# Sums of squares of the RMS norms: two float32r matmuls of a split operand in the place of one float32 matmul

## The chip, the cores and the metric

The kernel runs on one core of one Trainium2 chip. The core has a matrix engine (TensorE, shown as PE for its matmuls and PEld for the weight loads that go with them), a vector engine (VectorE, DVE), a scalar engine (ScalarE, ACT), GpSimd (POOL) and a queue engine (SyncE, SP) that issues most transfers. Matmuls write to PSUM, which has eight banks of 512 float32 columns; the rest works in SBUF, whose tiles have 128 partitions.

The metric is the device time of one execution in microseconds (us), as a median over runs. Before the change it is 1512.06 us (three runs, 1512.05 to 1512.68).

## The reference, cut to what matters

A two-layer transformer-like trunk on one sequence of 512 tokens with 1024 features. Each layer is a mixer, a cross-attention over a memory of 256 tokens, and a gated feed-forward block. What the change touches is the RMS norm that stands before each of these, over the memory, inside the mixers' heads, and at the end:

```python
def rms_norm(x, gain):
    x32 = x.astype(jnp.float32)
    y = x32 * lax.rsqrt(jnp.mean(x32 * x32, axis=-1, keepdims=True) + RMS_EPS)
    return (y * gain.astype(jnp.float32)).astype(x.dtype)
...
for layer in range(DEPTH):
    xn = rms_norm(x, mix_norm[layer])
    mixed = ...                              # layer 0: forgetting + differential attention; layer 1: mLSTM
    x = x + mixed
    x = x + memory_cross_attention(rms_norm(x, xattn_norm[layer]), rms_norm(mem, mem_norm[layer]), ...)
    x = x + conv_ffn(rms_norm(x, ffn_norm[layer]), ...)
return rms_norm(x, final_norm)
```

In layer 0 each of the four differential heads is normed over its 128 values, in layer 1 each of the four mLSTM heads over its 256 values.

## The kernel before, in words

**Layout.** The activations are held with features on partitions and tokens along the free dimension: `x` is eight tiles of 128 features by 512 tokens. So a norm is a sum over partitions and over the eight tiles. The tiles' squares are made on ScalarE and added up on VectorE into one tile `sq` (128x512; `squares`, L461 to L470). The sum over its partitions is a matmul. In `rsqrt_cols` (L390 to L396) each block of 128 tokens of `sq` is loaded as the weights, and a 128x2 tile of ones, `ones2`, is the moving operand; two equal columns of sums of 128 tokens come out in a PSUM bank. `rsqrt` (L398 to L411) makes the inverse root with some twelve VectorE instructions on 128x4 numbers: scale and epsilon (`z`, L404), a first guess from the bits, and three Newton steps (L408 to L410). `bcast_cols` (L413 to L435) spreads the result over all partitions: it splits it into two parts (L419 and `sub`, L259), builds two 128x512 diagonal tiles `sqt` on VectorE (L424), and multiplies them with ones on TensorE (L430), after which ScalarE copies the bank to `rb` (L434), where the caller wants it in SBUF. Projections run on the un-normed tiles meanwhile; `rb` multiplies their outputs when they leave PSUM.

**Precision.** Projections are exact to near float32 by splitting: `split` (L261) copies a value to float32r on ScalarE (the high part, L262), and VectorE subtracts it from the value (the low part, L259, also float32r). A product is then three float32r matmuls, high by high, high by low and low by high (`mm3`, L268 to L270; L329 to L331 in token-major form). Weights are split in this way as they arrive, 128x1024 at a time. The sums of squares are not split: `sq` and `ones2` are float32, and TensorE gets a float32 matmul. Attention scores times values and the mLSTM products are float32 too.

**Order.** Two planners written in Python decide at build time in which order the work is written down. `Plan` (L60) serves the mixers and the cross-attention: items carry a cost on TensorE, a priority, dependencies, resources (PSUM banks, weight buffers) and a chain of costs on ScalarE ("A") and VectorE ("D"); at each point the first ready item by priority goes next. `p_norm` (L347) adds a norm as two items: `one` (the sums and the inverse root) and `two` (the spread and what follows, `fin`). `x_norm` (L360) is that for `x`, and the memory norm, the four heads of layer 0 and the four of layer 1 call `p_norm` as well. `Sched` (L139) serves the feed-forward block with a queue per engine; its `norm` (L1186) adds `sums` (TensorE), `root` (VectorE) and `spread` (TensorE) with due times. The first norm of all (`first_sums`, L455) and the last (`finish`, L1683, through `rsqrt_cols`) are written out by hand. A scheduling layer below the planners then puts the instructions of each engine in their final order, by priority and by when it takes their operands to be ready, so that single broadcast matmuls (L430) stand inside a run of projection matmuls. Each engine executes its own list in order; semaphores make one engine wait for another.

**Where norms end up.** In layer 0's mixer the heads' results go to the output projection that begins after all heads. In layer 1's mixer the norm of `x` comes first, and a chain of small VectorE and ScalarE steps on 4x512 gate rows follows from `rb` (L552 to L587, with the scans L574 and L1464); TensorE's first use of that chain is a small transpose (L1473, of `cv` made at L1462). The last mLSTM head's norm is followed at once by the output projection, which multiplies by that head's split result (tiles `v`, made at L1619).

Of the kernel before, what the change touches and what calls it, by code (L numbers as in the profile page):

```python
# [10 lines left out]
F32R = mybir.dt.float32r  # L11
# [5 lines left out]
P = 128  # L17
SEQ = 512
# [41 lines left out]
class Plan:  # L60
# [11 lines left out]
    def add(self, fn, dur=0.0, deps=(), prio=None, take=(), free=(), chain=(), pre=(), after=0.0, order=(), load=(), st=None):  # L72
        it = Item(fn, dur, [d for d in deps if d is not None], len(self.items) if prio is None else prio, take, free, chain, pre, after, order, load, st)
        it.n = len(self.items)
        self.items.append(it)
        return it
# [141 lines left out]
class Builder:  # L218
# [128 lines left out]
    def p_norm(self, pl, state, n, done, scale, eps, fin, deps=(), prio=None, after=0.0, fdeps=(), chain=(("A", 0.5),)):  # L347

        st = {}

        def one():
            st["r"] = self.rsqrt_cols(state["sq"], n, scale, eps)

        def two():
            fin(st["r"], self.bcast_cols(st["r"], n, *done))

        a = pl.add(one, 0.4 * n / 512, deps, prio, take=("s",), free=("s",), chain=(("D", 2.3),), after=after)
        return pl.add(two, 0.5 * n / 512, [a, *fdeps], prio, take=("s",), free=("s",), chain=chain)

    def x_norm(self, pl, prio=0, after=0.0, deps=()):  # L360
# [22 lines left out]
    def evac_tok(self, ps, r, hi, lo):  # L383
# [2 lines left out]
        nc.scalar.activation(hi, ps, AF.Identity, scale=r)  # L386
        nc.vector.scalar_tensor_tensor(out=lo, in0=ps, scalar=r, in1=hi.bitcast(F32), op0=ALU.mult, op1=ALU.subtract)


    def rsqrt_cols(self, sq, n, scale, eps):  # L390

        nt = n // P
        ps = self.bank("b")
        for t in range(nt):
            self.nc.tensor.matmul(ps[:, 2 * t : 2 * t + 2], sq[:, t * P : (t + 1) * P], self.ones2[:], start=True, stop=True)  # L395
        return self.rsqrt(ps, nt, scale, eps)  # L396
# [722 lines left out]
    def ffn_steps(self, layer, mp):  # L1119
# [3 lines left out]
        nc, t = self.nc, self.t  # L1123
        sc = Sched(raw=3, h=3, s2=1, s4=1, a22=1, sum=1, hs=2, c=1, dr=2, v=1, u2=1, u3=1, act=10, acc=4, s=2, w=2)
        add = sc.add
# [4 lines left out]
        state = {}  # L1130
# [4 lines left out]
        def pe(dur, fn, deps, take=(), free=()):  # L1135
            clock[0] += dur
            return add("PE", dur, fn, deps, clock[0] - dur, take, free, 0.2)
# [48 lines left out]
        def norm():  # L1186
            prev = self.state
            st = {}
            n = {}

            def sums():
                n["ps"] = self.bank("s")
                for i in range(4):
                    nc.tensor.matmul(n["ps"][:, 2 * i : 2 * i + 2], prev["sq"][:, i * P : (i + 1) * P], self.ones2[:], start=True, stop=True)

            def root():
                self.r = self.rsqrt(n["ps"], 4, 1.0 / DM, EPS)

            def spread():
                self.rb = self.bcast_cols(self.r, SEQ, self.sp, "rb", 1)  # L1200

            a = pe(0.5, sums, (), [("s", st)])
            b = add("DVE", 2.3, root, [a], a.prio, (), [("s", st)])
            s2 = {}
            c = pe(0.5, spread, [b], [("s", s2)], [("s", s2)])
            return add("ACT", 0.7, None, [c], c.prio)
# [75 lines left out]
        def plain(p, fill):  # L1282
            st = {}
            at = clock[0]
            get = rows(st, at + 5.0)
            ready = []
            for j in range(2):
                b, last = block(t["up"][layer, 22 * j + p], KB8, own, clock[0], "acc", (), 2)

                def evac(j=j, b=b):  # L1290
                    nc.vector.tensor_tensor(out=st["hs_"][:, j, 2:514], in0=b["ps"][:], in1=self.rb[:], op=ALU.mult)

                if p == 0 and j == 0:
                    nonlocal normed
                    normed = norm()
                ready.append([add("DVE", 0.69, evac, [last, get, normed], clock[0] + 2.0, (), [("acc", b)])])
                fill()
            tail(p, st, ready, clock[0] + 3.0)
# [136 lines left out]
        if layer == 0:  # L1435
            for m in range(8):
                e = down(4, m, 2)
                a = add("ACT", 1.43, lambda m=m: self.xprep(m, "mix", 1, state), [e], clock[0] + 3.0)
# [368 lines left out]
```

## Time and profile before

| | |
|---|---|
| median of three runs | 1512.06 us (1512.05 to 1512.68) |
| profiled execution | 1512.78 us |
| its span in the trace | 1511.0 us |
| TensorE clock granted | 0.998 of full |
| TensorE busy | 1500.0 us (99%) |
| weight loads busy | 1281.7 us (85%) |
| VectorE busy | 1160.1 us (77%) |
| ScalarE busy | 774.8 us (51%) |
| GpSimd busy | 44.0 us (3%) |
| DMA | 146.52 MB, 97 GB/s in the mean |

The span runs from the first to the last instruction of the trace; the execution's own time is 1.8 us longer. Ends of matmuls are modelled, so that TensorE's 99% says that it hardly ever had nothing under way, not that it ran at its peak: what a matmul costs in a stream is the distance from its start to the start of the next. Matmul and weight load are separate records. A "form" such as `128*128 128x2 f32` is 128 rows by 128 columns of weights and an output of 128x2.

In time, by where the sums of the norms stand on TensorE: layer 0's mixer with its output projection takes the span up to 272 us, its cross-attention up to 420, its feed-forward block up to 774, layer 1's mixer up to 1003, its cross-attention up to 1151, and the rest is its feed-forward block with the final norm.

### The profile page before, as it was taken

What the parts mean: (1) busy time and instruction counts of PE and PEld (TensorE: products, weight loads), DVE (VectorE), ACT (ScalarE), POOL (GpSimd) and SP (SyncE); (2) the same over time, 40 slices, a digit from 0 to 9 for tenths busy, and PEclk for the clock granted to TensorE, in tenths of its full rate; (3) what the DMA queues carried; (4) which work ended last, traced back from release to release, by engine and by line L of the source; (5) the groups of instructions that cost most, each with busy time, mean ns of one, the idle gap of its engine ahead of it and who ended that gap; (6) DMA issues with size and microseconds to landing.
All of it is one profiled execution on the core that took longest, in us unless ns stands there. A gap on an engine that the chain in (4) does not pass through costs nothing.

```text
span 1511.0 us, 21313 instructions
## 1 busy us (share of the span) xinstructions
PE 1500.0 (99%) x8026; PEld 1281.7 (85%) x8026; DVE 1160.1 (77%) x2155; ACT 774.8 (51%) x1282; POOL 44.0 (3%) x118
## 2 busy tenths in 40 slices
PE   9999999999999999999999999999999999999998
PEld 8888888888888888988888778888888888888887
DVE  7889885766699788897678857666557988889864
ACT  6768564444465444454446634444445554444444
POOL 2000120000000000000001100000000000000000
PEclk9999999999999999999999999999999999999999
DMA  5222233323223333232222222332323332333322
GB/s 179 84 71 84 84 103 108 112 96 100 95 101 100 97 108 109 84 112 88 81 90 84 80 89 93 99 101 99 111 84 109 108 94 95 98 103 106 102 60 77
DMA packets 47480, 146.52 MB, mean 97 GB/s; under 512 B 5649, under 2 KB 5649, under 8 KB 47377
## 3 DMA queue, kind: packets, MB, share of 16 engines
q1 hardware_dynamic: 46368, 144.04, 29.4%
q8 instruction: 63, 1.03, 0.3%
q10 hardware_dynamic: 1008, 1.12, 0.2%
q14 instruction: 41, 0.33, 0.1%
HBM read 143.04 MB, written 2.10 MB: 96 GB/s over the span
## 4 chain that ended last, share of the span: by engine, by line
PE 92%; DVE 3%; ACT 2%; issue 1%; DMA 1%; POOL 0%; SPq 0%; DVEq 0%; POOLq 0%; ACTq 0%
PE acc L268 19%; PE acc L269 19%; PE acc L270 19%; PE w L269 5%; PE w L268 5%; PE w L270 5%; PE acc L330 2%; PE acc L331 2%; PE acc L329 2%; PE s L268 2%; PE s L269 2%; PE s L270 2%; PE w L1595 1%; PE w L681 1%; PE s L395 1%
## 5 line engine op out<-in xcount | busy, mean ns | idle before, releaser
L268 PE MATMUL acc<-xh,wh 128*128 128x512 f32 (+1 forms) x944 | 356.9, 378 | 0.0
L270 PE MATMUL acc<-xh,wl 128*128 128x512 f32 (+1 forms) x944 | 352.8, 374 | 0.0
L269 PE MATMUL acc<-xl,wh 128*128 128x512 f32 (+1 forms) x944 | 352.6, 374 | 0.0
L259 DVE TENSOR_TENSOR wl<-raw,wh 128x1024 fp32r<-128x1024 f32 (+2 forms) x215 | 258.0, 1200 | 51.9 <-ACT wh L262 38.1
L262 ACT CAST wh<-raw 128x1024 fp32r<-128x1024 f32 (+2 forms) x137 | 140.9, 1030 | 168.5 <-PE acc L269 99.6
L270 PEld LDWEIGHTS acc<-xh,wl 128*128 128x128 f32 x944 | 177.5, 188 | 31.7
L268 PEld LDWEIGHTS acc<-xh,wh 128*128 128x128 f32 x944 | 177.6, 188 | 30.4
L269 PEld LDWEIGHTS acc<-xl,wh 128*128 128x128 f32 x944 | 177.7, 188 | 30.3
L1254 DVE SCALAR_TENSOR_TENSOR c<-hs,vec,c 128x512 f32<-128x512 f32 x176 | 128.4, 746 | 7.4 <-ACT c L1247 6.8
L269 PE MATMUL w<-al,wh 128*128 128x512 f32 x304 | 118.5, 390 | 0.0
L268 PE MATMUL w<-ah,wh 128*128 128x512 f32 x304 | 118.5, 390 | 0.0
L270 PE MATMUL w<-ah,wl 128*128 128x512 f32 x304 | 118.3, 389 | 0.0
L1159 ACT CAST wh<-raw 128x1024 fp32r<-128x1024 f32 (+1 forms) x60 | 61.3, 1022 | 77.8 <-PE acc L269 49.3
L1247 ACT ACTIVATE c<-hs,vec 128x512 f32<-128x512 f32 x88 | 70.0, 812 | 40.2 <-DVE hs L1393 23.5
L495 DVE TENSOR_TENSOR x<-w,x 128x512 f32<-128x512 f32 x72 | 49.5, 687 | 31.9 <-PE w L270 31.6
L270 PEld LDWEIGHTS w<-ah,wl 128*128 128x128 f32 x304 | 57.1, 188 | 12.0
L268 PEld LDWEIGHTS w<-ah,wh 128*128 128x128 f32 x304 | 57.1, 188 | 10.9
L269 PEld LDWEIGHTS w<-al,wh 128*128 128x128 f32 x304 | 57.1, 188 | 10.7
L1159 ACT CAST wh<-dr 128x512 fp32r<-128x512 f32 x64 | 39.7, 620 | 47.9 <-issue 17.4
L1268 ACT CAST ah<-c 128x512 fp32r<-128x512 f32 x44 | 27.3, 620 | 68.9 <-DVE c L1264 68.9
L330 PE MATMUL acc<-wl,xh 128*128 128x256 f32 (+1 forms) x192 | 61.9, 323 | 0.2 <-DVE wl L259 0.2
L329 PE MATMUL acc<-wh,xh 128*128 128x256 f32 (+1 forms) x192 | 61.7, 326 | 0.0
(373 smaller groups left out, 3323.4 us busy)
## 6 DMA issues: line engine op xcount, KB each, us to landing
raw<-in_up_dram SPq DMA_DIRECT2D x88, 512.0 KB, 3.3
dr<-in_down_dram SPq DMA_DIRECT2D x64, 256.0 KB, 2.6
raw<-in_xk_dram SPq DMA_DIRECT2D x16, 512.0 KB, 3.3
raw<-in_wo_dram SPq DMA_DIRECT2D x16, 512.0 KB, 3.2
raw<-in_xq_dram SPq DMA_DIRECT2D x16, 512.0 KB, 3.3
raw<-in_xv_dram SPq DMA_DIRECT2D x16, 512.0 KB, 3.3
raw<-in_xo_dram SPq DMA_DIRECT2D x16, 512.0 KB, 3.3
raw<-in_down_dram SPq DMA_DIRECT2D x16, 384.0 KB, 3.0
```

Source lines behind the costliest of these rows:

```text
L259: self.nc.vector.tensor_tensor(out=lo, in0=v, in1=hi.bitcast(F32), op=ALU.subtract)
L262: self.nc.scalar.copy(hi, v)
L268: mm(out, wh, xh, start=first, stop=False, skip_group_check=parts)
L269: mm(out, wh, xl, start=False, stop=False, skip_group_check=parts)
L270: mm(out, wl, xh, start=False, stop=last, skip_group_check=parts)
L329: mm(ps, xh[k][:, ts], wh[:, ws], start=(k == 0), stop=False)
L330: mm(ps, xh[k][:, ts], wl[:, ws], start=False, stop=False)
L331: mm(ps, xl[k][:, ts], wh[:, ws], start=False, stop=(k == 7))
L495: self.nc.vector.tensor_tensor(out=self.x[m][:], in0=ps[:], in1=self.x[m][:], op=ALU.add)
L1159: nc.scalar.copy(st["wh"][:, :cols], st[tag][:, :cols])
L1247: nc.scalar.activation(st["c_"][:, j, :], hs()[:, j, 2:514], AF.Identity, scale=self.col("cw", (layer * 3 + 2) * 44 + blk), bias=self.col( ...
L1254: nc.vector.scalar_tensor_tensor(out=c, in0=hs()[:, j, n : n + 512], scalar=w, in1=c, op0=ALU.mult, op1=ALU.add)
```

## The change

The operand `sq` is split as the projections' operands are: `square_parts` makes two new single-buffered 128x512 tiles, `sqh` (ScalarE copy to float32r) and `sql` (VectorE subtraction). `part_sums` then gives for each block of 128 tokens two float32r matmuls into the same two columns, `sqh` and then `sql` as weights, with two columns of the float32r tile of ones `onesr` as the moving operand. In `p_norm` the split is an item `halved` of its own ahead of `one`, with a chain of a ScalarE and a VectorE cost, and `one` costs 0.5 instead of 0.4; in the feed-forward block a ScalarE task, an empty VectorE task and the sums stand in that order. The first norm and the two halves of the last still use float32. Last, `Bacc` is told a scratch size for dynamic DMA of 1024 bytes; without the argument it is 16384 bytes of each SBUF partition.

```diff
         st = {}
 
+        def halved():
+            st["sq"] = self.square_parts(state["sq"], n)
+
         def one():
-            st["r"] = self.rsqrt_cols(state["sq"], n, scale, eps)
+            st["r"] = self.rsqrt(self.part_sums(st["sq"], n, self.bank("b")), n // P, scale, eps)
...
-        a = pl.add(one, 0.4 * n / 512, deps, prio, take=("s",), free=("s",), chain=(("D", 2.3),), after=after)
+        a = pl.add(halved, 0, deps, prio, chain=(("A", 0.1 + 0.47 * n / 512), ("D", 0.14 + 0.54 * n / 512)), after=after)
+        a = pl.add(one, 0.5 * n / 512, [a], prio, take=("s",), free=("s",), chain=(("D", 2.3),), after=after)
         return pl.add(two, 0.5 * n / 512, [a, *fdeps], prio, take=("s",), free=("s",), chain=chain)
...
+    def square_parts(self, sq, n):
+
+        parts = [self.til(self.sp, tag, dtype=F32R, bufs=1) for tag in ("sqh", "sql")]
+        hi, lo = (p[:, :n] for p in parts)
+        self.split(hi, lo, sq[:, :n])
+        return hi, lo
+
+    def part_sums(self, parts, n, ps):
+
+        for t in range(n // P):
+            for i, p in enumerate(parts):
+                self.nc.tensor.matmul(ps[:, 2 * t : 2 * t + 2], p[:, t * P : (t + 1) * P], self.onesr[:, :2], start=i == 0, stop=i == 1)
+        return ps
...
+            def halved():
+                n["sq"] = self.square_parts(prev["sq"], SEQ)
+
             def sums():
-                n["ps"] = self.bank("s")
-                for i in range(4):
-                    nc.tensor.matmul(n["ps"][:, 2 * i : 2 * i + 2], prev["sq"][:, i * P : (i + 1) * P], self.ones2[:], start=True, stop=True)
+                n["ps"] = self.part_sums(n["sq"], SEQ, self.bank("s"))
...
-            a = pe(0.5, sums, (), [("s", st)])
+            a = add("ACT", 0.6, halved, (), 0.0)
+            a = add("DVE", 0.7, None, [a], 0.0)
+            a = pe(0.5, sums, [a], [("s", st)])
...
-    nc = _bacc.Bacc("TRN2", target_bir_lowering=False, num_devices=1)
+    nc = _bacc.Bacc("TRN2", target_bir_lowering=False, num_devices=1, dynamic_dma_scratch_size=1024)
```

## The prediction

> **What bounds the kernel now.** I read the page first, then the stretches, the sums' own lines, the timeline around them and the waits.
>
> ```profile
> span 1511.0 us, 21313 instructions
> ...
> PE 1500.0 (99%) x8026; PEld 1281.7 (85%) x8026; DVE 1160.1 (77%) x2155; ACT 774.8 (51%) x1282; POOL 44.0 (3%) x118
> ...
> PE 92%; DVE 3%; ACT 2%; issue 1%; DMA 1%; POOL 0%; SPq 0%; DVEq 0%; POOLq 0%; ACTq 0%
> ```
>
> TensorE is never long without work and carries 92% of the chain that ended last. So what counts is (a) the distance between matmul starts, where the change alters matmuls, and (b) new waits of TensorE. VectorE and ScalarE have room in the mean; by stretch (PE, PEld, DVE, ACT, POOL busy):
>
> ```profile
> 40.00:230.00 190.00, 189.06 (x1132) 161.04 (x1132) 157.93 (x480) 131.19 (x293) 18.07 (x32) 1.00 0.27 88
> 420.00:775.00 355.00, 355.00 (x1938) 308.58 (x1938) 298.81 (x451) 171.82 (x245) 2.79 (x23) 1.00 0.31 97
> 775.00:840.00 65.00, 64.29 (x278) 50.30 (x278) 50.44 (x89) 40.32 (x62) 6.59 (x12) 1.00 0.26 82
> ```
>
> Outside the start and the end TensorE idles 0.9 us in layer 0's heads and 0.7 us in layer 1's gate chain, and nothing in a feed-forward block. There is little to win from shorter waits, and any real wait put into this stream is lost.
>
> **The change, part by part. 1: the matmuls.** The sums' records:
>
> ```profile
> L395 PEld LDWEIGHTS s<-ones,sq x40: 186/192/192, 164.4 to 1502.7; 128*128 128x128 f32 x40
> L395 PEld LDWEIGHTS s<-ones,tb x32: 188/192/192, 99.7 to 155.1; 128*128 128x128 f32 x32
> L395 PEld LDWEIGHTS s<-ones,hsq x32: 188/192/192, 842.4 to 954.3; 128*128 128x128 f32 x32
> ...
> L1194 PEld LDWEIGHTS s<-ones,sq x16: 186/192/192, 420.0 to 1151.9; 128*128 128x128 f32 x16
> ```
>
> Four mLSTM heads of four token blocks give 16 float32 matmuls in the program and 32 `hsq` records here: one float32 matmul is two loads and two matmuls. The projections' float32r lines have one record for each. So 56 float32 matmuls (13 norms of four blocks, two memory norms of two) are 112 records now, and 112 float32r matmuls will be 112 records. What does one cost?
>
> ```profile
> 115.68 0.19 PEld L330 LDWEIGHTS acc<-wl,xh 128*128 128x128 f32 x1
> 115.80 0.19 PEld L331 LDWEIGHTS acc<-wh,xl 128*128 128x128 f32 x1
> ...
> 115.92 0.98 PEld L395 LDWEIGHTS s<-ones,tb 128*128 128x128 f32 x8
> ...
> 116.83 0.19 PEld L268 LDWEIGHTS acc<-xh,wh 128*128 128x128 f32 x1
> ```
>
> Eight float32 loads take 0.91 us from 115.92 to 116.83, 0.114 each: with two moving columns the load is the cost. Float32r loads just before are 0.12 apart, with 256 moving columns behind each, so a float32r load takes no more than 0.12. From below, the load's length by columns:
>
> ```profile
> L395 PEld LDWEIGHTS s<-ones,sq 128*128 128x128 f32 x40 | 5.2, 191 | 1.1 <-PE s L1657 0.4 <-issue 0.2 <-DVE sq L470 0.2
> ...
> L905 PEld LDWEIGHTS w<-pt,v 128*64 128x64 f32 x64 | 5.0, 136 | 4.8 <-issue 3.5 <-DVE sm L664 0.2
> ...
> L542 PEld LDWEIGHTS w<-xh,wh 128*100 128x100 f32 x8 | 1.3, 164 | 0.5
> ...
> L542 PEld LDWEIGHTS w<-xh,wh 128*40 128x40 f32 x8 | 0.9, 116 | 0.3
> ```
>
> Float32: (191 - 136) / 64 = 0.86 ns a column. Float32r: (164 - 116) / 60 = 0.80. The same rate within the rows' rounding, so 128 columns take between 0.102 and 0.12 us in float32r against 0.110 to 0.114. Over 112 records the difference lies between -1.3 and +1.0 us; I take 0. The matmuls are what the change is about, and they cost the same.
>
> A rule speaks otherwise. The Trainium skill, "FP8 and Floating Point Precision", section "TensorE Precision Notes", says that true float32 makes four passes through the array. By that alone two single passes would halve the sums' array work. The rows differ: with two moving columns the passes vanish beside the load, and the load is paid twice either way.
>
> **2: the split.** One copy on ScalarE and one subtraction on VectorE, as here:
>
> ```profile
> L259 DVE TENSOR_TENSOR al<-c,ah 128x512 fp32r<-128x512 f32 x44 | 30.3, 690 | 14.3 <-ACT ah L1268 13.8
> ...
> L1268 ACT CAST ah<-c 128x512 fp32r<-128x512 f32 x44 | 27.3, 620 | 68.9 <-DVE c L1264 68.9
> ```
>
> Thirteen times 0.62 and 0.69, and half of that twice for the memory: 8.7 us on ScalarE and 9.7 on VectorE, beside TensorE's stream. That costs nothing while the sums are not reached before `sql` is there; without this cover each norm would cost up to 0.62 + 0.69 and two handovers of some 0.07, 1.45 us.
>
> **3: the order.** Both planners know the longer chain and put the sums later. The built orders (no time is in them) show the same matmuls otherwise, moved about in layer 0's mixer from its third head on and in layer 1's mixer; a cross-attention and a feed-forward block differ only at their norm. Where cover is thin:
>
> *Cross-attentions.* 12 matmuls of 512 columns are drawn ahead of the sums. At 0.227 us (below) that is 2.7 us against 1.45: covered, 0. *Feed-forward norms.*
>
> ```profile
> 419.25 0.69 DVE L470 TENSOR_TENSOR sq<-sq,sqt 128x512 f32<-128x512 f32 x1
> 419.85 0.69 DVE L1224 TENSOR_TENSOR sum<-hs 128x512 f32<-128x512 f32 x1
> ...
> 421.08 0.16 DVE L404 TENSOR_SCALAR z<-s 128x4 f32<-128x4 f32 x1 [0.55 <-PE s L1194]
> ```
>
> `sq` is ready at 419.94, the sums start at 419.99. Now three matmuls come before the first and four more between it and the other seven, 1.6 us in all; `sql` stands behind L1224 and L1231 (0.69 and 0.4), so it ends about 421.75, and the seven come up at 421.65. 0.1 us each, 0.2 together; the bounds are 0 and the whole 1.45 each, and the value is near zero because these lines are the case itself. Everything queued behind `z` on VectorE comes 1.5 us later, which four accumulator banks hold off.
>
> *Layer 1's first norm.* Its chain feeds TensorE with no slack:
>
> ```profile
> 779.85 0.59 ACT L434 COPY rb<-s 128x512 f32<-128x512 f32 x1
> ...
> 794.07 0.39 PE L330 MATMUL acc<-wl,xh 128*128 128x512 f32 x1
> ...
> 794.30 0.39 PE L331 MATMUL acc<-wh,xl 128*128 128x512 f32 x1
> ...
> 794.45 0.68 DVE L1462 TENSOR_TENSOR cv<-cv,th 4x512 f32<-4x512 f32 x1
> ...
> 795.30 0.41 PE L1473 MATMUL s<-ident,cv 4*128 4x4 f32 x4
> ```
>
> `cv` is done at 795.13 and the transpose starts at 795.30: 0.17 us of slack. (Matmuls of 512 columns are 0.227 apart.) In the new order 17 more of them, 3.85 us, stand before the second broadcast matmul, but only seven, 1.6 us, before the transpose. If all of it reached `cv`, TensorE would wait 3.85 - 1.6 - 0.17 = 2.1 us. But weight subtractions of 1.2 us that stood in the chain are moved elsewhere, so the lower bound is 0. I take 0.6: the scheduling layer has placed such steps close to the time, as the waits show:
>
> ```profile
> PE s L430 <- DVE sqt L424: 0.3, 2, 0.2
> ...
> PEld s L430 <- DVE sqt L424: 3.1, 8, 0.6
> ```
>
> Of 32 broadcast matmuls eight wait, none of them over 0.6 us.
>
> *The last mLSTM head.* It is on the path, too:
>
> ```profile
> 962.78 1.29 DVE L259 TENSOR_TENSOR v<-num,v 128x512 fp32r<-128x512 f32 x2
> ...
> L268 PE MATMUL acc<-v,wh x10: 389/389/389, 963.5 to 982.3; 128*128 128x512 f32 x10
> ```
>
> Its first low part is ready about 963.4 and read at 963.8, 0.3 us of slack. The sums stand six matmuls later (1.36 us), and a weight subtraction that was in the root's steps now stands before them. The second broadcast is 0.6 us later by the orders: a wait of 0.2, between 0 and 1.2.
>
> *The other heads.* Their results are wanted much later; what can cost is the new order around them. I take +0.4, between -3 and +5 (the rivals' ends).
>
> *Scratch size.* Transfers are issued by SP and ACT; no wait for it shows. 0.
>
> The sum: 0 + 0 + 0.2 + 0.6 + 0.2 + 0.4 = +1.4. On the profiled execution's span of 1511.0 that is 1512.4, with the same 1.8 us around it 1514.2. That execution (1512.78) was 0.7 above the median of 1512.06, so I predict 1513.5 us.
>
> **The rivals.** *Slower: VectorE becomes the bound at the end of layer 0's heads.* There it is nearly full already:
>
> ```profile
> 200.00:210.00 10.00, 9.86 (x79) 9.10 (x76) 9.93 (x32) 7.50 (x19) 2.04 (x5) 1.00 0.29 96
> ...
> L664 DVE RECIPROCAL sm<-sm 128x1 f32<-128x1 f32 x64 | 9.2, 155 | 3.3 <-ACT x L663 2.5
> ...
> L657 DVE CUSTOM_DVE_ANT_0 x<-s,tb 128x512 f32<-128x512 f32 x8 | 5.5, 686 | 1.9 <-PE s L653 1.9
> L657 DVE DVE_READ_ACCUMULATOR2_ANT sm<- 128x1 f32 x64 | 5.2, 82 | 0.0
> ```
>
> In the new order the scores lag: at the point that is about 180 us in the trace before, 110 blocks of 128x128 scores have been issued instead of 121, and both orders have made up for it some 35 us later. Eleven blocks are 2.75 scores of 512 columns at 0.69 + 0.08 + 0.16 = 0.92 us: 2.5 us of VectorE, and with their scaling and copies up to about twice that, pressed into that stretch. As TensorE waits for the two score banks, it decides where that is more than VectorE's idle time. Price 2.5 to 5 us on top of 1.4: about 1517. For it: 9.93 of 10 in the row. Against: the planner counts VectorE's time, and drew projection matmuls forward for that reason.
>
> *Faster: float32r loads in half the time.* 112 x 0.056 = 6.3 us less and no waits: 1505.8. The Trainium skill, "TensorE: Matmul & The Clock Gate", section "Weight-path perf modes — Fast Weight Load (FWL) and DoubleRow", says that a faster load is on at 128 weights when the type is not FP32; were float32r such a type, this would be it. Against: equal rates per column above (though at fewer than 128 columns), and 128-column loads of both types are 0.19 long.
>
> *Faster: a luckier order.* If the waits of the broadcasts (3.1) and most of the mixers' 0.9 and 0.7 went, 1508 to 1509. Against: nothing in the change aims at them.
>
> **How the numbers follow.** About 0.2%, 3.0 us, is what a measurement of this kernel can tell from no change. The forecast, 1511 to 1515, has 0.50. The crowded stretch, or another new wait like it, has 0.38. The half-time loads have 0.05, the luckier order 0.07. So faster 0.12, same 0.50, slower 0.38. The range of 8 in 10 leaves out the half-time loads and the far ends of the others: 1508.5 to 1519.5.
>
> **What would show it.** Right: 112 records on the new line, about 0.11 us apart, and `sqh` and `sql` of 0.62 and 0.69 us with TensorE busy meanwhile. The waits table names L1473 or the broadcasts for less than 2 us. Wrong: records under 0.08 us apart, or TensorE's idle time between 40 and 230 us above 3 us.

## The result and the profile after

| | before | after |
|---|---|---|
| median of six runs each, taken side by side | 1512.40 us (1512.05 to 1513.70) | 1519.17 us (1518.23 to 1519.89) |
| profiled execution | 1512.78 us | 1518.23 us |
| its span | 1511.0 us | 1516.1 us |

The ratio is 1.0043, with a 95% interval of 1.0030 to 1.0056: the change costs 0.43%. The prediction's likeliest case was 1513.5 us; this is its slower case, and the range (1508.5 to 1519.5) holds it by only 0.3 us. The profiled execution is the fastest of the six, so the trace shows 5.1 us of the 6.8 between the medians.

First the page after the change: span, busy times, and the shares of the chain that ended last.

```profile
span 1516.1 us, 21341 instructions
...
PE 1503.0 (99%) x8026; PEld 1281.5 (85%) x8026; DVE 1168.9 (77%) x2170; ACT 782.6 (52%) x1297; POOL 41.5 (3%) x118
...
PE 92%; DVE 4%; ACT 2%; issue 1%; DMA 0%; SPq 0%; DVEq 0%; ACTq 0%
```

TensorE has the same 8026 records, and its busy time rose by 3.0 us all the same. Ends of matmuls are modelled, so a short wait behind a matmul is counted as busy. The stretches (PE, PEld, DVE, ACT, POOL busy) show the same blind spot:

```profile
40.00:230.00 190.00, 188.13 (x1117) 159.43 (x1116) 158.83 (x483) 131.92 (x297) 16.15 (x32) 1.00 0.25 83
420.00:775.00 355.00, 354.85 (x1933) 307.79 (x1932) 301.31 (x455) 174.25 (x251) 2.78 (x23) 1.00 0.30 96
775.00:840.00 65.00, 63.47 (x277) 49.96 (x276) 49.33 (x85) 38.62 (x59) 5.99 (x12) 1.00 0.27 89
```

In layer 0's heads TensorE seems to idle 1.9 us in place of 0.9. That is 1.0 us, and the real loss there is three times as much. It shows when starts of matmuls are compared in the two traces, at points where both orders have issued the same set of matmuls. The difference of the two starts is the delay so far; between two such points it tells where time went. (Up to 143.2 and 144.6 us the sets agree, but the last matmul isn't the same one in both; these rows are good to 0.1 us.)

| up to (time before, us) | delay after the change | gained or lost since the line above |
|---|---|---|
| 24.5, start | -0.27 | |
| 143.2, in layer 0's heads | +1.03 | +1.30 |
| 144.6 | +1.58 | +0.55 |
| 235.0, end of the heads | +3.13 | +1.55 |
| 419.7, after the cross-attention | +2.94 | -0.19 |
| 429.9, first feed-forward norm | +3.37 | +0.43 |
| 783.2, layer 1's mixer begins | +3.23 | -0.14 |
| 800.5, first transposes of its gates | +4.81 | +1.58 |
| 849.7 | +4.19 | -0.62 |
| 968.0, after the last mLSTM head | +4.72 | +0.53 |
| 1150.8, after the cross-attention | +4.71 | -0.01 |
| 1161.9, second feed-forward norm | +5.13 | +0.42 |
| 1504.0 | +5.13 | 0.00 |

The sums themselves are as forecast. The first lines are the sums' line by tile (count, shortest/median/longest in ns), then the split's, then the first head's eight matmuls in the timeline:

```profile
L405 PEld LDWEIGHTS s<-ones,sqh x56: 186/192/192, 104.6 to 1158.0; 128*128 128x128 f32 x56
...
L405 PEld LDWEIGHTS s<-ones,sql x56: 187/192/192, 104.7 to 1158.1; 128*128 128x128 f32 x56
...
L262 ACT CAST sqh<-tb x4: 611/620/643, 101.4 to 153.4; 128x512 fp32r<-128x512 f32 x4
L259 DVE TENSOR_TENSOR sql<-tb,sqh x4: 683/690/695, 102.0 to 154.2; 128x512 fp32r<-128x512 f32 x4
```

```profile
104.70 0.17 PE L405 MATMUL s<-ones,sqh 128*128 128x2 f32 x1
104.72 0.25 PE L405 MATMUL s<-ones,sql 128*128 128x2 f32 x1
...
105.39 0.25 PE L405 MATMUL s<-ones,sql 128*128 128x2 f32 x1
105.51 0.36 PE L329 MATMUL acc<-wh,xh 128*128 128x256 f32 x1
```

112 records, the eight of a norm take 0.81 us from 104.70 to 105.51 (0.81 before, from 99.83 to 100.64), and the split's parts take 0.62 and 0.69 us. What TensorE waited for between 40 and 235 us, before and then after (total, times, longest, in us):

```profile
PEld s L430 <- DVE sqt L424: 0.8, 2, 0.5
PEld s L652 <- ACT ka L622: 0.6, 1, 0.6
...
PEld s L652 <- DVE sm L657: 0.4, 1, 0.4
```

```profile
PEld s L448 <- DVE sqt L442: 1.5, 3, 0.7
PEld s L670 <- DVE sm L675: 1.0, 3, 0.5
PEld s L670 <- DVE sm L682: 0.8, 1, 0.8
PE s L448 <- DVE sqt L442: 0.8, 2, 0.5
PEld s L448 <- issue: 0.6, 1, 0.6
PEld s L670 <- ACT ka L640: 0.6, 1, 0.6
```

Two kinds have grown: the spreads of the heads' inverse roots (L448, L430 before), and scores (L670, L652 before) that wait for VectorE. The largest single one lies inside an attention group. The weights' queue shows it first, then TensorE:

```profile
202.95 0.19 PEld L670 LDWEIGHTS s<-ka,qa 128*128 128x128 f32 x1 [0.81 <-DVE sm L682]
```

```profile
201.94 1.07 PE L923 MATMUL w<-pt,v 128*64 128x512 f32 x2
202.95 0.44 PE L670 MATMUL s<-ka,qa 128*128 128x384 f32 x1
203.23 0.34 PE L671 MATMUL s<-kb,qa 128*128 128x384 f32 x1
203.50 2.37 PE L923 MATMUL w<-pt,v 128*64 128x512 f32 x14
205.79 0.33 PE L699 MATMUL w<-ident,x 128*128 128x128 f32 x1
```

A group of sixteen multiplies the weights of two heads with their values, each head on 64 columns of the array, and the two halves run side by side: their starts come in pairs. In the new order a pair of scores stands between the first half's opening matmul and the second's, and it has to wait 0.81 us for VectorE, which has work without a gap over 0.05 us from 199.3 to 203.5 us. The group takes 3.85 us, 0.55 of it the scores; the like one before takes 2.47 (198.52 to 200.99). That is 0.83 us lost. In the other three groups nothing changed (2.30 or 2.31 us).

In layer 1's gate chain the wait at the transposes is there:

```profile
PEld s L1494 <- issue: 1.9, 1, 1.9
PE s L1494 <- DVE cv L1483: 1.5, 1, 1.5
```

And in the feed-forward block the first spread waits. These are VectorE's steps from `z` to the first `sqt`, after the change, and TensorE's matmuls there:

```profile
425.60 0.16 DVE L422 TENSOR_SCALAR z<-s 128x4 f32<-128x4 f32 x1 [0.73 <-PE s L405]
...
426.70 1.23 DVE L259 TENSOR_TENSOR wl<-raw,wh 128x1024 fp32r<-128x1024 f32 x1
427.84 0.16 DVE L427 TENSOR_TENSOR a<-a,zh 128x4 f32<-128x4 f32 x1
427.91 1.22 DVE L259 TENSOR_TENSOR tl<-sum,th 128x1024 fp32r<-128x1024 f32 x1
...
431.24 0.69 DVE L442 TENSOR_TENSOR sqt<-ident,rh 128x512 fp32r<-128x512 f32 x1
```

```profile
431.44 0.39 PE L269 MATMUL acc<-xl,wh 128*128 128x512 f32 x1
431.98 0.50 PE L448 MATMUL s<-sqt,ones 128*128 128x512 f32 x1
```

The two starts are 0.54 us apart, where matmuls of this length are 0.227 apart: 0.31 us are lost, and 0.11 more behind the spread, whose successor starts at 432.32. Low parts of weights and tiles, 1.2 us each, stand between steps of 0.16, and the root takes 6.3 us from `z` to the end of `sqt` (425.60 to 431.93). That is no news. Before the change it took as long, from the 421.08 of the prediction's row to 427.47, and the spread stood 0.34 us behind it:

```profile
426.78 0.69 DVE L424 TENSOR_TENSOR sqt<-ident,rh 128x512 fp32r<-128x512 f32 x1
```

```profile
427.81 0.39 PE L430 MATMUL s<-sqt,ones 128*128 128x512 f32 x1
```

Less the delay of 2.95 us that was there already, the root now ends 1.5 us later, since the sums do; the spread was moved back by four matmuls, 0.9 us, only. 1.5 - 0.9 - 0.34 leaves 0.3 us, which is the wait. Why the spread was moved by no more isn't shown. The sums themselves lose nothing here: they wait for `sqh` as long as they waited for `sq` before. The weights' queue at the first of them, before and after:

```profile
419.99 0.97 PEld L1194 LDWEIGHTS s<-ones,sq 128*128 128x128 f32 x8 [0.34 <-DVE sq L470]
```

```profile
423.58 0.19 PEld L405 LDWEIGHTS s<-ones,sqh 128*128 128x128 f32 x1 [0.31 <-ACT sqh L262]
```

### The profile page after: what moved, and what is told of

It reads as the page before. It is cut to its first block, busy times and chain, and to the rows that moved or that the text cites. A ratio compares the mean times of both kernels' runs of the same rounds, so it can differ in the third digit from the quotient of the medians.

```text
span 1516.1 us, 21341 instructions
## 1 busy us (share of the span) xinstructions
PE 1503.0 (99%) x8026; PEld 1281.5 (85%) x8026; DVE 1168.9 (77%) x2170; ACT 782.6 (52%) x1297; POOL 41.5 (3%) x118
## 3 DMA queue, kind: packets, MB, share of 16 engines
q8 instruction: 63, 1.03, 0.3%
## 4 chain that ended last, share of the span: by engine, by line
PE 92%; DVE 4%; ACT 2%; issue 1%; DMA 0%; SPq 0%; DVEq 0%; ACTq 0%
PE acc L268 20%; PE acc L269 19%; PE acc L270 19%; PE w L268 5%; PE w L269 5%; PE w L270 5%; PE acc L329 2%; PE acc L330 2%; PE acc L331 2%; PE s L268 2%; PE s L270 2%; PE s L269 2%; PE w L1616 1%; PE s L405 1%; PE w L923 1%
```

## The experiments

All are beside runs of the kernel before on the same chip. Delays are read at common matmuls, as above, and given net of the delay at 24.5 us, which differs by up to 1.5 us from one execution to the next (last section).

**1. The heads alone.** In the changed kernel `p_norm` takes an argument `parts`; where it is false, the norm has the float32 matmul and the old numbers. So have all norms here but those of layer 0's four differential heads (the callers not shown likewise).

```diff
-        self.memnorm = self.p_norm(pl, state, MEM, (mp, "memrb", 1), 1.0 / DM, EPS, fin, done[7], 1)
+        self.memnorm = self.p_norm(pl, state, MEM, (mp, "memrb", 1), 1.0 / DM, EPS, fin, done[7], 1, parts=False)
...
-            norm = self.x_norm(pl, 0, after=5.0)
+            norm = self.x_norm(pl, 0, after=5.0, parts=False)
```

> The change is made at the four norms of layer 0's differential heads alone; all other norms keep the float32 matmul. In the two traces the changed kernel stands 3.2 us behind the kernel before at the matmul that is at 210 us before, 0.4 to 0.5 more at each feed-forward norm and 1.4 more at layer 1's first norm. Theory A (the heads' part is a cost of its own): 3.0 behind by 215 us and nothing added after, a span of 1513.5 to 1514.5 and about 1515.4 us. Rival B (the losses depend on each other, and what is lost in the heads is in part caused by the other norms, the memory's among them): under 1.5 us behind at 215 us, about 1513.5 us. The prediction had +0.4 here, between -3 and +5.

Measured: 1516.65 us against 1513.46, ratio 1.0021 (1.0011 to 1.0030). The delay grows by 1.3 us up to 143 us and by 3.34 up to 235, and after that it stays within 0.2. Theory A: the heads cost 3.3 us by themselves, as much as in the changed kernel (3.40).

**2. All but the heads.** The reverse.

```diff
-                f = self.p_norm(pl, sq, SEQ, (), 1.0 / P, EPS, scaled, [w], p + SOFT_PRIO, chain=(("D", 0.66),))
+                f = self.p_norm(pl, sq, SEQ, (), 1.0 / P, EPS, scaled, [w], p + SOFT_PRIO, chain=(("D", 0.66),), parts=False)
```

> The changed kernel, but the four norms of layer 0's differential heads keep the float32 matmul and the old numbers. The heads alone cost 3.2 us beside the kernel before. Theory A (the costs add): 5.9 - 3.2 = 2.7 us left, between layer 1's first norm (1.4 to 1.6) and the feed-forward norms (0.4 to 0.5 each): about 1515.2 us, less than 0.5 us behind at 210 us. Rival B (the memory norm's split alone is enough to upset the order there): over 1.5 us behind at 210 us and 1516.5 us or more.

Measured: 1515.69 us against 1513.69, ratio 1.0016 (1.0007 to 1.0026). The net delay is -0.2 us at 235; 0.4 are lost at each feed-forward norm, 1.6 at the transposes and 0.4 at the last mLSTM head, and 2.0 us are left at the end. With the heads' 3.34 that makes 5.3, and the changed kernel has 5.40: the costs add. The memory's norm, which is split here, upsets nothing.

**3. All but layer 1's first norm.**

```diff
-            norm = self.x_norm(pl, 0, after=5.0)
+            norm = self.x_norm(pl, 0, after=5.0, parts=False)
```

> The changed kernel, but layer 1's first norm keeps the float32 matmul and the planner's old numbers for it. In the changed kernel TensorE waits 1.5 us for the cell gates' cv at the transposes there, and 1.4 us are lost between 429 and 797 us beside the 0.4 of the feed-forward norm's. Theory A: the wait goes back to nothing (0.17 us of slack before) and 1.3 to 1.6 us are gained there, all of it kept to the end; about 1517.6 us. Rival B: the wait is caused by what came before (the later start of the stretch, other weights in flight) and stays above 1 us; then nothing is gained.

Measured: 1517.39 us against 1512.70, ratio 1.0030 (1.0019 to 1.0041). Between 783 and 800.5 us nothing is lost, where the changed kernel loses 1.58; the wait for `cv` on TensorE's matmuls is gone, and the end stands 3.8 us behind in place of 5.4. Theory A.

**4. The order alone.** The planners' new items stay, the work is the old one.

```diff
     def square_parts(self, sq, n):
-        parts = [self.til(self.sp, tag, dtype=F32R, bufs=1) for tag in ("sqh", "sql")]
-        hi, lo = (p[:, :n] for p in parts)
-        self.split(hi, lo, sq[:, :n])
-        return hi, lo
+        return sq
...
-            for i, p in enumerate(parts):
-                self.nc.tensor.matmul(ps[:, 2 * t : 2 * t + 2], p[:, t * P : (t + 1) * P], self.onesr[:, :2], start=i == 0, stop=i == 1)
+            self.nc.tensor.matmul(ps[:, 2 * t : 2 * t + 2], parts[:, t * P : (t + 1) * P], self.ones2[:], start=True, stop=True)
```

> The planners' new numbers and the order that follows from them stay, but the work is the old one: no split, float32 matmuls. Theory A (the new order of the matmuls and of VectorE's work costs, not the split): 2.5 to 3.2 us behind at the matmul of 210 us, about 1 to 1.4 more at the transposes of layer 1's gates, and about 1517 us. Rival B (the split's 0.62 and 0.69 us in the chain cost): under 1 us behind at 210 us, nothing at the gates, and 1512.5 to 1514 us.

Measured: 1518.11 us against 1513.46, ratio 1.0031 (1.0019 to 1.0043). Without any split the heads lose 2.4 of the 3.4 us, the same 1.5-us wait stands at the transposes, and the score pair stands in the same group, which takes 3.85 us again. Only the feed-forward norms lose nothing. Theory A for the mixers, where the order is the greater part; what is left for the split, by difference, is about 1.0 us in the heads and all of the feed-forward norms' 0.85. There 30 matmuls stand between the last sum and the first spread, as before the change; in the changed kernel it is 27, so the split alone makes the scheduling layer draw the spread nearer.

**5. The work alone.** The split and the new matmuls, issued as one piece by the old items.

```diff
-        a = pl.add(halved, 0, deps, prio, chain=(("A", 0.1 + 0.47 * n / 512), ("D", 0.14 + 0.54 * n / 512)), after=after)
-        a = pl.add(one, 0.5 * n / 512, [a], prio, take=("s",), free=("s",), chain=(("D", 2.3),), after=after)
+        a = pl.add(one, 0.4 * n / 512, deps, prio, take=("s",), free=("s",), chain=(("D", 2.3),), after=after)
...
-            a = add("ACT", 0.6, halved, (), 0.0)
-            a = add("DVE", 0.7, None, [a], 0.0)
-            a = pe(0.5, sums, [a], [("s", st)])
+            a = pe(0.5, sums, (), [("s", st)])
```

(`one` and `sums` call `square_parts` themselves.)

> The split and the float32r matmuls of the change with the planners' old numbers, so in the old order: the split is issued when the sums are. This takes the cover away from the split. The prediction priced that at up to 1.45 us for a norm of 512 columns: eleven of these and two of half the size are at most 17.4 us, about 1530 us, if every sum waits in full. Theory A (order is the cost, and the split is covered only because the order was changed): waits of TensorE at the sums of 0.7 to 1.5 us at most norms, 1520 to 1530 us. Rival B (the old order has slack of its own for the split): waits at few norms, and under 1515 us; then the change of order is a needless loss.

Measured: 1517.57 us against 1513.46, ratio 1.0028 (1.0017 to 1.0039). Neither theory: 4.3 us are lost, of which 2.5 in the heads, 0.4 at each feed-forward norm, 0.8 in layer 1's heads, nothing at the transposes. (The text counts eleven norms of 512 columns; there are thirteen, so the bound was 20.3 us.) The whole price of the missing cover is paid once, at the first head:

```profile
PEld s L402 <- ACT sqh L262: 2.5, 6, 1.4
PE s L402 <- ACT sqh L262: 1.2, 1, 1.2
PEld s L402 <- DVE sql L259: 0.7, 2, 0.5
```

So the old order left slack before most sums. Telling the planners of the longer chain saved that one wait of 1.2 to 1.4 us and made others of 2.4 us in the heads and 1.6 at the transposes: the heads lose 3.4 us with it and 2.5 without.

**6. The halves of a group exchanged.** On the changed kernel, for the attention group at 202 us.

```diff
-                        for s in range(2):
+                        for s in (1, 0):
```

> The changed kernel, but in the forgetting attention's weighting the two heads of a pair are written down in the other order (s = 1 before s = 0), so that the half whose operand is ready last comes first and the score pair that stands inside the second group of the changed kernel no longer separates the halves. In the changed kernel that group takes 3.85 us, of which about 0.55 is the score pair, and the like group before takes 2.48. Theory A (the two 64-column halves run side by side only while their matmuls alternate, and the score pair put them out of step): the group takes 2.3 to 2.5 us, and the kernel gains 0.8 to 0.9 us on the changed one at the next common matmul, about 1518 us in the median. Rival B (the group only shows a wait that comes anyway): no gain behind it.

Measured: 1519.58 us against 1512.70, ratio 1.0041 (1.0026 to 1.0056). The score pair still stood between the halves, and the group took 3.85 us again. So the edit did not make the case that the two theories were about; it says only that the pair comes there whichever half is first.

**7. Halves out of step.** On the kernel before.

```diff
-                    for j in range(4):
-                        at = 1024 if j == 3 else 640 * j
-                        for s in range(2):
+                    for j, s in ((0, 0), (1, 0), (0, 1), (2, 0), (1, 1), (3, 0), (2, 1), (3, 1)):
+                            at = 1024 if j == 3 else 640 * j
```

> The kernel before, with the eight float32 matmuls of each forgetting-attention group written down out of step: the first head's half is one block ahead of the second's, so that blocks of different length alternate. In the traces so far a group takes 2.30 us when the two halves start together, 2.47 when the second starts 0.17 us later, 3.68 when it starts 0.64 later, and 3.85 with a score pair of 0.55 between. Theory A (the halves overlap only while equal blocks stand beside each other): each of the four groups takes 3 to 3.7 us, 3 to 5.5 us more in all, which TensorE's stream shows in full: 1515.5 to 1518 us. Rival B (the lag is only waiting for an operand, and the halves overlap in any order): 2.3 to 2.6 us a group and no change of the time.

Measured: 1513.02 us against 1513.69, ratio 0.9998 (0.9988 to 1.0009). The groups take 2.36, 2.47, 2.36 and 2.35 us. Rival B: blocks of any length overlap, and what a group loses is the time by which its second half is late. (The 3.68 us in the expectation, from experiment 8, held 0.68 of a wait behind the group; its matmuls took 3.01.) In the changed kernel the second half is late because the pair that waits for VectorE stands ahead of it in TensorE's list.

**8. A longer root in the plan.** The planner's number for the heads' root is raised.

```diff
-        a = pl.add(one, 0.5 * n / 512, [a], prio, take=("s",), free=("s",), chain=(("D", 2.3),), after=after)
+        a = pl.add(one, 0.5 * n / 512, [a], prio, take=("s",), free=("s",), chain=(("D", root),), after=after)
...
-                f = self.p_norm(pl, sq, SEQ, (), 1.0 / P, EPS, scaled, [w], p + SOFT_PRIO, chain=(("D", 0.66),))
+                f = self.p_norm(pl, sq, SEQ, (), 1.0 / P, EPS, scaled, [w], p + SOFT_PRIO, chain=(("D", 0.66),), root=4.0)
```

> The changed kernel, with 4.0 us in place of 2.3 as the planner's number for the inverse root's VectorE time of layer 0's four heads. In the changed kernel that root took 4.6 us for the first head (105.5 to 110.1 us), because a weight's low part, memory low parts and the next head's sql stand between its steps, and the spread's matmuls wait 0.3 to 0.6 us four times. Theory A (the planner's number is too small, so the spreads are drawn too early): the waits of the spreads in the heads fall below 0.5 us in all and 1 to 1.5 us are gained by 210 us. Rival B (any other order of this crowded stretch has its own waits): the waits move to the scores or to the turned blocks, and the loss at 210 us stays between 2 and 4 us.

Measured: 1519.12 us against 1512.70, ratio 1.0039 (1.0024 to 1.0054). The net delay is 0.3 us at 143 and 3.4 from 236 on, as in the changed kernel. Rival B: up to 143 us a microsecond less is lost, and as much more later. (The 210 us of the expectation are no common point here.)

**9. The root on GpSimd.**

```diff
-            nc.vector.tensor_tensor(out=a, in0=y, in1=y, op=ALU.mult)
-            nc.vector.tensor_tensor(out=a, in0=a, in1=zh, op=ALU.mult)
-            nc.vector.scalar_tensor_tensor(out=y, in0=a, scalar=1.5, in1=y, op0=ALU.add, op1=ALU.mult)
+            nc.gpsimd.tensor_tensor(out=a, in0=y, in1=y, op=ALU.mult)
+            nc.gpsimd.tensor_tensor(out=a, in0=a, in1=zh, op=ALU.mult)
+            nc.gpsimd.tensor_scalar(out=a, in0=a, scalar1=1.5, scalar2=None, op0=ALU.add)
+            nc.gpsimd.tensor_tensor(out=y, in0=a, in1=y, op=ALU.mult)
```

> The changed kernel, with the three Newton steps of the inverse root on GpSimd (twelve instructions on 128x4) in place of VectorE (nine), where low parts of 0.7 to 1.2 us stand between them in the changed kernel and stretch a root to 4.6 us in a head and 6.3 us in the feed-forward block. Theory A (the spreads wait because VectorE's bulk work stretches the root): TensorE's waits of the spreads for sqt, 4.6 us in the changed kernel, fall below 2 us, and 1.5 to 3 us are gained. Rival B (the scheduling layer places the spreads by its own times, whatever the engine; or GpSimd's small instructions take as long): the waits stay above 3.5 us or move to other lines, and under 1 us is gained.

Measured: 1548.54 us against 1513.69, ratio 1.0235 (1.0220 to 1.0250). The waits for `sqt` grew tenfold, from 4.6 us in the changed kernel. The first two rows are TensorE's waits, the last is one of the steps on GpSimd (busy us, mean ns):

```profile
PEld s L449 <- DVE sqt L443: 26.6, 20, 3.0
PE s L449 <- DVE sqt L443: 21.6, 14, 2.6
```

```profile
L426 POOL TENSOR_TENSOR a<-y 128x4 f32<-128x4 f32 (+1 forms) x54 | 16.2, 300 | 434.0 <-DVE zh L424 431.3
```

A step takes 0.22 to 0.30 us there, against 0.16 on VectorE. But a longer root is the smaller part. In the feed-forward block the root takes 6.9 us in place of 6.3, while the scheduling layer has drawn the spread nearer: 19 matmuls stand between the last sum and the first spread, 27 in the changed kernel. Those eight are 1.8 us, and TensorE stops 2.5 us there. So theory A fails, and rival B's first half holds: the layer places the spreads by its own times. What a root free of low parts would gain stays untried.

**10. The scratch size alone**, on the kernel before.

```diff
-    nc = _bacc.Bacc("TRN2", target_bir_lowering=False, num_devices=1)
+    nc = _bacc.Bacc("TRN2", target_bir_lowering=False, num_devices=1, dynamic_dma_scratch_size=1024)
```

> The kernel before with the smaller scratch alone. The prediction has 0 for it: 1512 to 1514 us and no wait that is not there before. Rival (addresses of the tiles move and something reads or writes slower): over 1 us in either direction.

Measured: 1513.58 us against 1512.70, ratio 1.0001 (0.9992 to 1.0010). Nothing. One thing in it matters for the table above: at 833 us this trace gains 0.6 us, where a score in the trace before starts 1.02 us behind the matmul ahead of it and here 0.47. Nothing was changed near that place, and the traces of the other experiments there lie between 0.2 lost and 0.6 gained, so the -0.62 in the table is no merit of the change.

**11. One matmul for a block, no split.** The kernel before and its order; the instructions that form `sq` write it as float32r.

```diff
-            nc.vector.tensor_tensor(out=state["sq"][:, :n], in0=state["sq"][:, :n], in1=tmp[:, :n], op=ALU.add)
+            nc.vector.tensor_tensor(out=state["sq"][:, :n].bitcast(F32R), in0=state["sq"][:, :n], in1=tmp[:, :n], op=ALU.add)
...
-            st["r"] = self.rsqrt_cols(state["sq"], n, scale, eps)
+            ps = self.bank("b")
+            for t in range(n // P):
+                self.nc.tensor.matmul(ps[:, 2 * t : 2 * t + 2], state["sq"][:, t * P : (t + 1) * P].bitcast(F32R), self.onesr[:, :2], start=True, stop=True)
+            st["r"] = self.rsqrt(ps, n // P, scale, eps)
```

(The other writers of summed squares, and the feed-forward block's sums, likewise.)

> The kernel before, with its order, whose sums of squares are written as float32r by the instruction that forms them and summed by one float32r matmul for each block: no low part (the squares are rounded to float32r, which leaves out what the split keeps) and 56 records fewer. If a record costs its load, 0.112 us, as the prediction has it, and TensorE's stream is the bound there: 56 x 0.112 = 6.3 us less, about 1506 us. Rival: the time saved turns into waits for VectorE and ScalarE behind the sums: 1509 to 1512 us.

Measured: 1507.05 us against 1513.46, ratio 0.9958 (0.9944 to 0.9973), faster than both kernels.

```profile
span 1505.3 us, 21201 instructions
...
PE 1494.5 (99%) x7970; PEld 1276.0 (85%) x7970; DVE 1158.7 (77%) x2155; ACT 774.7 (51%) x1282; POOL 42.7 (3%) x118
```

56 records fewer, and the span is 5.7 us shorter than in the trace before: 0.10 us a record. So a sum's load with its matmul of two columns has this price, in float32 and float32r alike, and the way to less is fewer of them.

**12. Both.** The kernel of 11 with the root of 9.

> The kernel with squares as float32r and one matmul for each block, and the Newton steps on GpSimd. Alone the first took 1507.05 us. Theory A: the waits for sqt of about 3 us that it keeps from the kernel before shrink by half and VectorE has 1.3 us less for each norm: 1505 to 1506.5 us. Rival B: the new order of the crowded stretches costs as it did in the changed kernel: 1507 to 1511 us.

Measured: 1533.80 us against 1513.69, ratio 1.0125 (1.0106 to 1.0145). Both expectations fail, by what made 9 slow: in the feed-forward block 14 matmuls stand between the last sum and the first spread, 30 in experiment 11, and TensorE stops 2.0 us there.

## Why the prediction was wrong in its likeliest case

*The matmuls: 0.* Right. 112 records, 0.112 us apart, and the sums' eight take the 0.81 us that they took before. The half-time load is refuted: the float32r rows above are 0.112 us apart, as far as those of float32 before. The Trainium skill, "TensorE: Matmul & The Clock Gate", section "Weight-path perf modes — Fast Weight Load (FWL) and DoubleRow", has the faster load on at 128 weights when the type is not FP32; the trace shows no such gain for float32r. Experiment 11 confirms the price from the other side.

*The split: 0 beside TensorE's stream.* Right in the mixers for the sums themselves, which wait nowhere there; its durations are as forecast. The price without the cover, 1.45 us a norm, is what the one uncovered sum of experiment 5 pays (1.2 to 1.4); the other norms had cover in the old order, too.

*Cross-attentions: 0.* Right: -0.19 and -0.01.

*Feed-forward norms: 0.1 each.* Measured 0.43 and 0.42, inside the bounds, four times the value, and not at the sums, where it was put. The step that failed is the sentence that everything behind `z` comes 1.5 us later and four accumulator banks hold that off. No wait shows for VectorE's other readers behind it; but the spread stands in TensorE's own list, 0.34 us behind the root. That number could have been read before.

*Layer 1's first norm: 0.6.* The mechanism, the place and the bounds (0 to 2.1) were right, the size was not: 1.58, with a wait of 1.5 us in the matmuls' row. Of the prediction's 3.85 us about 3.35 (1.6 + 0.17 + 1.58) reached `cv`. The argument for a small value, that the scheduling layer places such steps close to the time, rested on the waits of the broadcasts; that they are short says nothing of the transposes, which stand at the other end of the chain.

*The last mLSTM head: 0.2.* Inside the bounds, at twice the value: 0.4 between 963.5 and 968 us.

*The other heads' new order: 0.4, between -3 and +5.* This is the term that failed: +3.4. By experiment 4 the order alone makes 2.4 of it, which leaves about 1.0 for the split. In the trace it is made of spreads at 111, 113, 128 and 165 us (0.3 to 0.6 us each by the distance of starts), a score at 146 us (0.5), and the attention group at 202 us (0.8); of the gaps of 0.3 to 0.4 us that the kernel before had at 171, 194 and 202 us one is left. How much belongs to each can't be settled to the tenth, since the two orders share few points in between. The term was given its value because these heads' results are wanted much later; but it is not only the last readers that TensorE waits for. The spreads and the scores stand in its list, and what stands behind them waits, too. The bounds (-3 to +5) were wide enough, and it is these that let the range hold the result; the value in them was a guess.

*The slower rival.* Its time (1517) is nearer the mark than the forecast, and its place is right in part. Its mechanism holds for one wait: the score at 202 us, 0.8 of the 3.4, waits for VectorE. The rest of it is not what happened, for VectorE is not fuller there: from 145 to 215 us it was busy 61.8 us before and 58.7 after. What came is the other half of the case that had 0.38, "another new wait like it", in several places.

*What would show it.* The waits named L1494 for 1.5 us, under the 2 of the sign, but the spreads for 4.6 over the whole trace (3.7 in the weights' queue, 0.9 on the matmuls). That sign could not have told: before the change they had 3.4. TensorE's idle time between 40 and 230 us was 1.9, under the 3 that was to mark the forecast as wrong, so this sign said "right" while 3.4 us were lost. Idle time taken from modelled ends was the wrong measure; starts of the same matmuls would have been the right one.

## What to carry to other kernels

Where an engine has work for its whole span, giving a planner a truer, longer chain for a small step moves that step and everything around it, and the new order has waits of its own: price the order by every instruction that stands in the busy engine's list, also those whose results are wanted late. Measure a chain of tiny steps from its first to its last start in the trace, with what other work stands between them, and look whether its reader stands close behind. And a matmul with two moving columns costs its weight load: fewer loads help, another type with as many does not.

## What the runs showed of the hardware

**A short stop of TensorE can halve its clock for more than three microseconds.** With the order alone (experiment 4) TensorE stopped 1.51 us for the transposes, and this follows (PE, PEld, DVE, ACT, POOL busy, then the granted clock):

```profile
801.00:802.00 1.00, 1.00 (x6) 0.85 (x6) 0.97 (x3) 0.09 (x1) 0.00 (x0) 0.98 0.00 0
802.00:803.00 1.00, 1.00 (x3) 0.73 (x3) 1.00 (x3) 0.97 (x2) 0.00 (x0) 0.50 0.04 8
803.00:804.00 1.00, 1.00 (x4) 0.80 (x3) 0.97 (x2) 0.94 (x3) 0.00 (x0) 0.50 0.00 0
804.00:805.00 1.00, 1.00 (x4) 0.81 (x3) 0.96 (x2) 0.47 (x1) 0.00 (x0) 0.50 0.28 45
805.00:806.00 1.00, 1.00 (x5) 0.79 (x5) 0.18 (x1) 0.00 (x0) 0.00 (x0) 0.82 0.83 295
```

About 3.4 us at half the clock cost as much again as the wait: that trace loses 3.18 us between 783 and 800.5 us (in the time of the trace before), the changed kernel's 1.58. The changed kernel has the same stop and kept its clock in the profiled execution:

```profile
802.00:803.00 1.00, 1.00 (x6) 0.85 (x6) 0.97 (x3) 0.09 (x1) 0.00 (x0) 1.00 0.00 0
803.00:804.00 1.00, 1.00 (x6) 0.80 (x6) 1.00 (x3) 0.97 (x2) 0.00 (x0) 1.00 0.00 0
```

It did not in each of its runs, as the mean clock of the runs suggests. The five kernels with this stop (the changed one and experiments 2, 4, 6 and 8) had a mean clock of 0.996 in 9 of 30 runs; the kernel before and experiments 1, 3, 5, 7, 10 and 11 in none of 101 (9 and 12, which wait at most norms, aside). The Trainium skill, "TensorE: Matmul & The Clock Gate", section "What's actually happening", has the clock fall to half after an idle window of about 3.4 us. The length of the half-clock stretch agrees with such a window; that the engine must stop as long does not, since 1.51 us was enough here, in some executions. In each trace the granted clock changes only on a grid of 3.413 us, and where a stop falls on this grid may decide. In experiment 4 it lies inside one step (799.2 to 800.7 us, the step ends at 801.95), and the next step has half the clock; in the changed kernel and in experiments 2 and 8 a border of the grid cuts the stop in two, and the clock stays. But in experiment 6 a stop of 1.51 us inside one step left the clock alone, so the rule stays open.

**Half clock at the start sets the spread of the runs.** TensorE stops there for 1.3 to 1.4 us in every trace, and then has half the clock for one step of 3.4 us or for two, somewhere between 18 and 26 us. (No trace is without this stop, so that it is the cause is inferred from the case above.) The changed kernel's stop, and the stretch from 18 to 24 us in it and with the smaller scratch alone (experiment 10):

```profile
16.79 0.42 PE L561 MATMUL w<-xl,wh 128*40 128x512 f32 x1 [1.27 <-DVE xl L494]
```

```profile
18.00:24.00 6.00, 6.00 (x38) 5.66 (x39) 4.52 (x16) 1.05 (x1) 0.00 (x0) 0.72 0.33 100
```

```profile
18.00:24.00 6.00, 6.00 (x32) 5.66 (x32) 3.95 (x13) 1.22 (x2) 0.00 (x0) 0.56 0.23 69
```

A mean clock of 0.72 in the one and 0.56 in the other, which stood 1.5 us behind the kernel before from there on. The four traces with two steps (experiments 1, 3, 6 and 10) stand 1.3 to 1.5 us behind the kernel before at 24.5 us, the others at most 0.6. This is the 1.5 us by which runs of one kernel differ, so for effects of a microsecond or two I trusted starts of common matmuls more than medians. At equal mean clock (0.998) the changed kernel's three runs have a median of 1518.33 us; those of the kernel before beside the experiments lie between 1511.9 and 1513.1. So of the 6.8 us between the medians roughly 1 is such clock, and 5.4 are the delays of the table, from -0.27 to +5.13; 0.3 stand outside the span, where the profiled execution has 2.1 us after and 1.8 before.
